# A row sum bound by its loads: all loads issued by SyncE, row buffers and the last runs on aligned addresses

## The chip, the core and the metric

The kernel runs on one core of one Trainium2 chip. The metric is device time in microseconds (us); the lower, the better. The times of before are 160.58, 160.60 and 160.58 us, with a median of 160.58 us.

## The reference

```python
# x: float32 [32, 512, 1024]
def reference(x):
    return np.sum(x, axis=-1).astype(np.float32)
```

The input is 16,384 rows of 1,024 numbers, 64 MiB in all. The output is one number for each row, 64 KiB.

## The kernel before, in words

The 16,384 rows are seen as 128 partitions with 128 rows each (`J = 128`). They are loaded 16 rows per partition at a time (`BIG = 16`), which is 64 KiB in each partition and 8 MiB in all, into three row buffers `rows_0` to `rows_2` that are used in turn. `rows_0` begins at byte 16,512 of each partition, which lies 128 bytes past a multiple of 256; the other two follow at distances of 65,536 bytes. The source of every partition's piece begins at a whole row, so at a multiple of 4,096 bytes.

The order of the work is written out by hand:

1. **The first load** (line 97) brings eight rows per partition, 4 MiB. SyncE (SP) issues it at the program's entry, ahead of the barrier between the engines.
2. **Seven loads of 8 MiB** (`g` from 0 to 6, line 99) follow. GpSimd (POOL) issues them with `single_packet=True`. From `g = 2` on POOL first waits on the semaphore `summed`, which VectorE (DVE) raises when it has summed the block that lies in the buffer to be filled again.
3. **The last eight rows** come as four runs, issued by POOL (line 99) once `summed` shows that their buffer is free. Run 0 is rows 1 to 5 and the first 484 numbers of row 6. Run 1 is row 7 and the first 774 numbers of row 8. Run 2 is the rest of row 6 (540 numbers) and run 3 the rest of row 8 (250 numbers). Runs 2 and 3 land in the small tensor `ends`, runs 0 and 1 in a row buffer. The runs' semaphores are called `five`, `seventh`, `sixth` and `eighth`.

Each load has a semaphore of its own, which reaches 16 when all of it has landed.

DVE sums the first load and loads 0 to 5 with one reduction each (`vec`, line 106). The last big load is split: DVE sums ten of its rows with `halves` (line 115, which adds the two halves of a row and accumulates), and ScalarE (ACT) sums six (`act`, line 135). Of the last eight rows ACT takes three. Rows 6 and 8 are summed in two steps: the part that landed first goes into one element of `ends`, and a second `halves` adds that element, the rest of the row and a zero. Two zeros are written at the start by one strided memset (line 170).

ACT stores the results of the first 112 rows per partition (lines 210 and 211); SP waits for DVE (`done`) and ACT, issues the last store (line 227) and waits until it has landed (line 228).

Of the kernel before, what the change touches and what calls it, by code (L numbers as in the profile page):

```python
# [30 lines left out]
def kernel(  # L31
# [5 lines left out]
    nc = tc.nc  # L37
# [7 lines left out]
    fp32 = mybir.dt.float32  # L45
    P = 128
    batch, seq, dim = x.shape
# [18 lines left out]
    def rows_from(j, n):  # L66
        if j < ONE:
            return x_a[:, j : j + n, :]
        return x_b[:, j - ONE : j - ONE + n, :]

    last = J // BIG - 1
    tail = last * BIG
    FIRST = 8

    bufs = [
        ctx.enter_context(nc.sbuf_tensor(f"rows_{k}", [P, BIG * dim], fp32))
        for k in range(3)
    ]
    sums = ctx.enter_context(nc.sbuf_tensor("sums", [P, J], fp32))
    SIXTH, EIGHTH = 484, 774  # L80
    ends = ctx.enter_context(
        nc.sbuf_tensor("ends", [P, 2 * dim - SIXTH - EIGHTH + 4], fp32)
    )
    unread = [
        ctx.enter_context(nc.psum_tensor(f"unread_{k}", [P, dim], fp32)) for k in range(4)
    ]
# [1 line left out]
    def semaphore(name):  # L88
        return ctx.enter_context(nc.semaphore(name=name))

    def block_of(t, a, n):
        return t[:, a * dim : (a + n) * dim].rearrange("p (n d) -> p n d", d=dim)

    def load(dst, src, k):
        sem = semaphore(f"load_{k}")
        if k == "first":
            nc.sync.dma_start(out=dst, in_=src).then_inc(sem, 16)
        else:
            nc.gpsimd.dma_start(out=dst, in_=src, single_packet=True).then_inc(sem, 16)  # L99
        return sem  # L100

    summed = semaphore("summed")

    def vec(j, block):
        n = block.shape[1]
        return nc.vector.tensor_reduce(  # L106
            out=sums[:, j : j + n],
            in_=block,
            axis=mybir.AxisListType.X,
            op=mybir.AluOpType.add,  # L110
        )

    def halves(dst, src):
        n = src.shape[-1] // 2
        return nc.vector.tensor_tensor_reduce(  # L115
            out=src[:, :n],
            in0=src[:, :n],
            in1=src[:, n:],
            scale=1.0,
            scalar=0.0,  # L120
            op0=mybir.AluOpType.add,
            op1=mybir.AluOpType.add,
            accum_out=dst,
        )
# [21 lines left out]
    t = bufs[0]  # L146
    block = block_of(t, 0, FIRST)
    landed = load(block, rows_from(tail, FIRST), "first")
    loads = [(landed, tail, block)]
    for g in range(last):  # L150
        t = bufs[(1 + g) % 3]
        if g > 1:
            nc.gpsimd.wait_ge(summed, g - 1)
        block = block_of(t, 0, BIG)
        loads.append((load(block, rows_from(g * BIG, BIG), g), g * BIG, block))

# [7 lines left out]
    rows5, left6 = block_of(t, 0, 5), t[:, 5 * dim : 5 * dim + SIXTH]  # L164
    c = 6 * dim
    row7, left8 = t[:, c : c + dim], t[:, c + dim : c + dim + EIGHTH]
    six = dim - SIXTH + 2
    whole6, whole8 = ends[:, :six], ends[:, six:]
    right6, right8 = whole6[:, 1:-1], whole8[:, 1:-1]
    nc.vector.memset(ends[:, six - 1 :: whole8.shape[-1]], 0.0)  # L170
    for landed, first, block in loads[:-1]:
        nc.vector.wait_ge(landed, 16)
        vec(first, block).then_inc(summed, 1)
    nc.gpsimd.wait_ge(summed, last - 1)
    line = rows_from(j, 8).rearrange("p n d -> p (n d)")
    runs = ((t[:, : 5 * dim + SIXTH], 0), (t[:, c : c + dim + EIGHTH], 6 * dim),
            (right6, 5 * dim + SIXTH), (right8, 7 * dim + EIGHTH))
    five, seventh, sixth, eighth = (
        load(dst, line[:, at : at + dst.shape[-1]], f"run_{k}")
        for k, (dst, at) in enumerate(runs)  # L180
    )
# [5 lines left out]
    carried = semaphore("carried")  # L187
    landed, first, block = loads[-1]
# [7 lines left out]
    n_early = n_acts  # L196

    nc.vector.wait_ge(five, 16)
    halves(whole6[:, :1], left6).then_inc(carried, 1)
    for q in range(3):  # L200
        halves(sum_of(q), rows5[:, q, :])
    for q in range(3, 5):
# [10 lines left out]

    done = semaphore("done")
    nc.vector.wait_ge(seventh, 16)
    halves(whole8[:, :1], left8).then_inc(carried, 1)
    nc.vector.wait_ge(sixth, 16)
    nc.vector.wait_ge(carried, 1)
    halves(sum_of(5), whole6)
# [39 lines left out]
```

## Time and profile before

| | |
|---|---|
| median of the runs | 160.58 us |
| span of the profiled execution, first to last instruction | 159.6 us |
| median minus span | 0.98 us |
| DVE busy | 121.6 us, 42 instructions |
| ACT busy | 11.0 us |
| POOL busy | 6.2 us |
| DMA traffic | 67.18 MB, mean 421 GB/s over the span |

The profiled execution has no time of its own beside its span: the span runs from the first to the last instruction, and what a run takes before and after it is not in the profile. The 0.98 us are therefore the difference between that span and the median of the runs.

In the profile, a DMA queue's "share of 16 engines" is the time that its packets took, divided by the length of the stretch and by 16, since every load is spread over 16 DMA engines. A packet is put down to the stretch in which it starts. "q0 software_dynamic" is the queue of the loads that POOL issues, "q1 hardware_dynamic" that of SP's DMAs, "q10" that of ACT's.

### The profile page before, as it was taken

The numbers are of one execution on the slowest core, as the hardware profiler recorded it, in microseconds if no ns is written. First come the engines' busy times: TensorE is split into PE (matmuls) and PEld (weight loads), VectorE is DVE, ScalarE is ACT, GpSimd is POOL, SyncE is SP. The second block draws the span as 40 slices with busy tenths as digits, with TensorE's granted clock in tenths as the row PEclk, the third lists the DMA queues.
The fourth block names the chain that finished last, engine by engine and source line by source line (L and its number), as shares of the span: only waits on it lengthen the run. The fifth ranks groups of instructions, "written<-read, shape, count | busy, mean of one in ns | idle before, by whom it ended". The sixth has DMA issues, their size and how long they took to land.

```text
span 159.6 us, 123 instructions
## 1 busy us (share of the span) xinstructions
DVE 121.6 (76%) x42; ACT 11.0 (7%) x19; POOL 6.2 (4%) x15
## 2 busy tenths in 40 slices
DVE  0000008999998999949999499986999679995986
ACT  3000000000000000000000000000000000000995
POOL 3000000010001000010000100010000220000000
DMA  7999996996997979969969969969969979898993
GB/s 263 526 394 394 435 600 279 526 509 279 526 444 345 526 345 444 526 279 509 526 263 526 526 263 526 509 279 526 509 279 526 460 329 526 378 411 364 438 402 127
DMA packets 2000, 67.18 MB, mean 421 GB/s; under 512 B 624, under 2 KB 624, under 8 KB 848
## 3 DMA queue, kind: packets, MB, share of 16 engines
q0 software_dynamic: 1424, 62.92, 91.2%
q1 hardware_dynamic: 288, 4.20, 6.6%
q10 hardware_dynamic: 288, 0.06, 0.2%
HBM read 67.11 MB, written 0.07 MB: 421 GB/s over the span
## 4 chain that ended last, share of the span: by engine, by line
DMA 74%; DVE 22%; POOL 1%; issue 1%; POOLq 0%
DMA rows<-in_x_dram 56%; DVE sums L106 22%; DMA ends<-in_x_dram 19%; POOL rows L99 1%; DVE ends L115 0%; DVE sums L115 0%; POOLq L43 0%
## 5 line engine op out<-in xcount | busy, mean ns | idle before, releaser
L106 DVE TENSOR_REDUCE sums<-rows 128x16 f32<-128x16384 f32 (+1 forms) x7 | 111.9, 15999 | 32.2 <-DMA rows<-in_x_dram 32.2
L135 ACT ACTIVATE unread<-rows 128x1024 f32<-128x1024 f32 x9 | 9.1, 1013 | 145.5 <-DMA rows<-in_x_dram 145.5
L115 DVE CUSTOM_DVE_ANT_0 rows<-rows 128x512 f32<-128x512 f32 (+2 forms) x15 | 9.0, 659 | 2.6 <-DMA rows<-in_x_dram 2.6
L99 POOL DMA_DIRECT2D rows<-in_x_dram x9 | 4.9, 546 | 122.4 <-DVE sums L106 120.9
L135 ACT ACTIVATION_READ_ACCUMULATOR unread<-rows 128x1 f32 x9 | 1.7, 186 | 0.0
L135 ACT ACT_TABLE_LOAD x1 | 1.3, 1283 | 1.4 <-PEq L43 1.4
L170 DVE MEMSET ends<- 128x2 f32 x1 | 0.1, 60 | 1.5 <-PEq L43 1.5
L115 DVE DVE_READ_ACCUMULATOR2_ANT sums<- 128x1 f32 x15 | 1.2, 80 | 0.0
L99 POOL DMA_DIRECT2D ends<-in_x_dram x2 | 1.1, 543 | 0.0
L115 DVE CUSTOM_DVE_ANT_0 ends<-ends 128x271 f32<-128x271 f32 (+1 forms) x2 | 0.7, 364 | 0.1
L115 DVE DVE_READ_ACCUMULATOR2_ANT ends<- 128x1 f32 x2 | 0.2, 84 | 0.0
L243 POOL MEMSET const-float32-0.0<- 128x1 f32 x1 | 0.1, 99 | 0.2 <-issue 0.2
L243 POOL MEMSET const-bfloat16-1.0<- 128x1 bf16 x1 | 0.1, 103 | 0.0
L243 POOL MEMSET const-float32-1.0<- 128x1 f32 x1 | 0.1, 99 | 0.0
L243 POOL MEMSET const-uint8-127<- 128x1 uint8 x1 | 0.1, 99 | 0.0
## 6 DMA issues: line engine op xcount, KB each, us to landing
rows<-in_x_dram SPq DMA_DIRECT2D x1, 4096.0 KB, 24.5
rows<-in_x_dram POOLq DMA_DIRECT2D x1, 2802.0 KB, 27.9
rows<-in_x_dram POOLq DMA_DIRECT2D x1, 899.0 KB, 29.6
ends<-in_x_dram POOLq DMA_DIRECT2D x1, 270.0 KB, 29.7
ends<-in_x_dram POOLq DMA_DIRECT2D x1, 125.0 KB, 29.5
rows<-in_x_dram POOLq DMA_DIRECT2D x7, 40.5
out_dram<-sums ACTq DMA_DIRECT2D x1, 48.0 KB, 1.6
out_dram<-sums ACTq DMA_DIRECT2D x1, 8.0 KB, 1.5
```

What stands on the lines that cost most here:

```text
L99: nc.gpsimd.dma_start(out=dst, in_=src, single_packet=True).then_inc(sem, 16)
L106: return nc.vector.tensor_reduce(out=sums[:, j : j + n], in_=block, axis=mybir.AxisListType.X, op=mybir.AluOpType.add,)
L115: return nc.vector.tensor_tensor_reduce(out=src[:, :n], in0=src[:, :n], in1=src[:, n:], scale=1.0, scalar=0.0, op0=mybir.AluOpType.add, op ...
L135: nc.scalar.activation(out=unread[n_acts % len(unread)][:, :], in_=src, func=mybir.ActivationFunctionType.Copy, accum_out=sums[:, j : j + ...
L170: nc.vector.memset(ends[:, six - 1 :: whole8.shape[-1]], 0.0)
L243: nc = _bacc.Bacc("TRN2", target_bir_lowering=False, num_devices=1)
```

## The change

SP issues all loads, plain, without `single_packet`; the waits on `summed` that stood ahead of the loads move from POOL to SP with them. A tensor named `unused` fills the space up to the next multiple of 4,096 bytes, so that the row buffers begin at byte 20,480. The runs are cut at 512 and 768 numbers instead of 484 and 774; `ends` now lies directly behind the row buffers, the piece of row 8 in it begins 64 numbers (256 bytes) behind the end of that of row 6, and the partial sum and the zero stand behind each piece instead of around it. The two zeros are written by two memsets.

```diff
+    taken = (nc.sbuf_base + 31) // 32 * 32
+    ctx.enter_context(nc.sbuf_tensor("unused", [P, -taken % 4096], mybir.dt.uint8))
     bufs = [ ... ]
+    SIXTH, EIGHTH = 512, 768
+    PAD = 64
+    ends = ctx.enter_context(
+        nc.sbuf_tensor("ends", [P, 2 * (dim + PAD) - SIXTH - EIGHTH], fp32)
+    )
     sums = ctx.enter_context(nc.sbuf_tensor("sums", [P, J], fp32))
-    SIXTH, EIGHTH = 484, 774
-    ends = ctx.enter_context(
-        nc.sbuf_tensor("ends", [P, 2 * dim - SIXTH - EIGHTH + 4], fp32)
-    )
...
     def load(dst, src, k):
         sem = semaphore(f"load_{k}")
-        if k == "first":
-            nc.sync.dma_start(out=dst, in_=src).then_inc(sem, 16)
-        else:
-            nc.gpsimd.dma_start(out=dst, in_=src, single_packet=True).then_inc(sem, 16)
+        nc.sync.dma_start(out=dst, in_=src).then_inc(sem, 16)
         return sem
...
-            nc.gpsimd.wait_ge(summed, g - 1)
+            nc.sync.wait_ge(summed, g - 1)
...
-    six = dim - SIXTH + 2
-    whole6, whole8 = ends[:, :six], ends[:, six:]
-    right6, right8 = whole6[:, 1:-1], whole8[:, 1:-1]
-    nc.vector.memset(ends[:, six - 1 :: whole8.shape[-1]], 0.0)
+    n6, n8 = dim - SIXTH, dim - EIGHTH
+    right6, right8 = ends[:, :n6], ends[:, n6 + PAD : n6 + PAD + n8]
+    whole6, whole8 = ends[:, : n6 + 2], ends[:, n6 + PAD : n6 + PAD + n8 + 2]
+    left_sums = [w[:, -2:-1] for w in (whole6, whole8)]
+    for w in (whole6, whole8):
+        nc.vector.memset(w[:, -1:], 0.0)
...
-    nc.gpsimd.wait_ge(summed, last - 1)
+    nc.sync.wait_ge(summed, last - 1)
...
-    halves(whole6[:, :1], left6).then_inc(carried, 1)
+    halves(left_sums[0], left6).then_inc(carried, 1)
...
-    halves(whole8[:, :1], left8).then_inc(carried, 1)
+    halves(left_sums[1], left8).then_inc(carried, 1)
```

In bytes per partition the four runs were 22,416, 7,192, 2,160 and 1,000; they become 22,528, 7,168, 2,048 and 1,024. Both add up to 32,768.

## The prediction

> **What bounds the kernel now.** I read the page first: its lines on DVE, DMA, the queues and the chain.
>
> ```profile
> span 159.6 us, 123 instructions
> DVE 121.6 (76%) x42; ACT 11.0 (7%) x19; POOL 6.2 (4%) x15
> ...
> DMA  7999996996997979969969969969969979898993
> ...
> DMA packets 2000, 67.18 MB, mean 421 GB/s; under 512 B 624, under 2 KB 624, under 8 KB 848
> ...
> q0 software_dynamic: 1424, 62.92, 91.2%
> q1 hardware_dynamic: 288, 4.20, 6.6%
> ...
> DMA 74%; DVE 22%; POOL 1%; issue 1%; POOLq 0%
> ```
>
> The two load queues together hold the 16 DMA engines for 97.8% of the span. DVE is busy 76% of it. The chain names DVE for 22%, so the timeline has to tell whether DVE ever holds up a load.
>
> ```profile
> 0.00 0.38 SPq L97 DMA_DIRECT2D rows<-in_x_dram  x1
> ...
> 1.94 1.20 POOL L99 DMA_DIRECT2D rows<-in_x_dram  x2 [1.50 <-POOLq L43]
> 24.48 8.69 DVE L106 TENSOR_REDUCE sums<-rows 128x8 f32<-128x8192 f32 x1 [22.91 <-DMA rows<-in_x_dram]
> ...
> 70.43 17.22 DVE L106 TENSOR_REDUCE sums<-rows 128x16 f32<-128x16384 f32 x1 [2.13 <-DMA rows<-in_x_dram]
> ...
> 126.65 1.05 POOL L99 DMA_DIRECT2D rows<-in_x_dram  x2 [18.82 <-DVE sums L106]
> 127.69 1.08 POOL L99 DMA_DIRECT2D ends<-in_x_dram  x2
> ...
> 147.84 0.69 DVE L115 CUSTOM_DVE_ANT_0 rows<-rows 128x512 f32<-128x512 f32 x1 [2.13 <-DMA rows<-in_x_dram]
> ...
> 157.44 0.44 DVE L115 CUSTOM_DVE_ANT_0 ends<-ends 128x271 f32<-128x271 f32 x1
> ...
> 157.81 0.28 DVE L115 CUSTOM_DVE_ANT_0 ends<-ends 128x126 f32<-128x126 f32 x1
> ...
> 158.13 0.35 SPq L227 DMA_DIRECT2D out_dram<-sums  x1
> ```
>
> It does not. From 70.43 to 147.84 DVE starts four new blocks after the first, always on a landing, so an 8 MiB load takes (147.84 - 70.43) / 4 = 19.35 us, and DVE needs only 17.22 us for it. The last four loads are issued from 126.65 on, 21 us ahead of the landing at 147.84 of the load before them. At 19.35 us for 8 MiB, 64 MiB take 154.8 us; the remaining 4.8 us of the span are the start (the first packets) and the end (last landing, a 0.28 us sum, the store).
>
> Next, single packets, picked out with the DMA view over narrow stretches. In this order the stretches are 0 to 2 us; 5.9 to 6.0; 6.53 to 6.6; 147.4 to 153.4 (run 0); 153.5 to 155.5 (run 1).
>
> ```profile
> q1 hardware_dynamic: 16, 0.52, 96.6%
> ```
> ```profile
> q1 hardware_dynamic: 1, 0.03, 75.8%
> ```
> ```profile
> q0 software_dynamic: 2, 0.13, 432.1%
> ```
> ```profile
> q0 software_dynamic: 112, 2.51, 97.7%
> ```
> ```profile
> q0 software_dynamic: 131, 0.85, 102.0%
> ```
>
> One 32 KiB packet on SP's queue took 0.758 x 16 x 0.1 = 1.213 us, one 64 KiB packet on POOL's 4.321 x 16 x 0.07 / 2 = 2.420 us. Eight of the latter are 19.36 us, the whole period of a load: the packets stand end to end, on one queue, without a gap. Two of the former are 2.426 us, so a packet costs 6 ns beside its bytes, and 2.414 us per 64 KiB, or 36.8 ns per 1,000 bytes, is the rate. The first 16 packets took 0.966 x 2 = 1.93 us each, 0.72 us over the later ones.
>
> **The change part by part.** The sum is made against the span of 159.6 us plus the 0.98 us that separate it from the median, 160.58 us.
>
> *Loads 0 and 1 move to SP's queue.* SP issues them behind its own first load, after the barrier, where POOL did it at 1.94. The first load's eight packets per engine last until about 1 + 1.93 + 7 x 1.21 = 11.4 us, so an issue at 2 us is covered by 9 us: 0. With one queue the first load no longer shares the engines with load 0. It lands near 12 us instead of 24.48, DVE's first sum ends near 21 instead of 33.17, and load 2 is issued earlier. Behind that stand loads 0 and 1, 38 us of transfer, so nothing ends earlier by it: 0.
>
> *The later issues and their waits.* SP now waits for `summed` and issues at 0.38 us a load, where POOL took about 0.53.
>
> ```profile
> POOL rows L99 <- DVE sums L106: 120.9, 6, 30.3
> DVE sums L106 <- DMA rows<-in_x_dram: 32.2, 6, 22.9
> ```
>
> POOL idled 120.9 us on those waits, so they are slack, and on SP nothing else is queued behind them but the final store, due at 158.13, while the last wait ends near 126.4: 0. If the 21 us of cover were gone, a load would start late by DVE's sum; nothing here shortens it.
>
> *64 KiB packets on SP's queue.* The trace shows that queue with 32 KiB packets alone. If it keeps 64 KiB whole: 0. If it halves them, 7 loads x 8 packets = 56 more per engine at 6 ns cost +0.34 us. I take 0, since SP's queue carried the first load's 32 KiB pieces whole.
>
> *Aligned row buffers.* Packets now land 128 bytes past a multiple of 256. The bounds: nothing, or all 6 ns of 56 + 8 + 16 = 80 packets per engine, -0.48 us. The nearest rows are runs 0 and 1, whose ends are crooked too. Run 0: 0.977 x 6 x 16 / 112 = 0.837 us, by the line 22,416 bytes plus 6 ns are 0.832. Run 1: 13 of the 131 are completion writes (under 512 bytes); leaving those 9 ns each, (1.020 x 2 x 16 - 0.12) / 118 = 0.276 against 0.271. So a crooked end costs 5 ns, and run 0 and run 1 regain 16 x 5 ns = -0.08 us. For the shifted begin I take a third of the 6 ns, as part of them must be what any packet costs: -0.14 us.
>
> The Trainium skill (DMA: Bandwidth & Descriptors, section How a descriptor splits into AXI transactions) says that a piece not starting at a multiple of 256 bytes pays the 32-byte beats from the boundary below it. By it a shift of 128 bytes costs 4 beats on 2,048, 0.2% of the transfer, an estimate of -0.3 us when it goes; that lies inside the bounds above, and no run so far shows an aligned load.
>
> *Runs 2 and 3 as single packets.* The page has 848 - 624 = 224 packets from 2 to 8 KB: run 1's 128, so 96 for the 256 pieces of runs 2 and 3, which POOL's queue grouped. On SP's queue each piece is probably a packet: (256 - 96) / 16 = 10 more per engine at 6 ns, +0.06 us. The bytes of the four runs stay.
>
> *The end.* Landing and completion:
>
> ```profile
> ends<-in_x_dram POOLq DMA_DIRECT2D x1, 270.0 KB, 29.7
> ends<-in_x_dram POOLq DMA_DIRECT2D x1, 125.0 KB, 29.5
> ...
> out_dram<-sums SPq DMA_DIRECT2D x1, 8.0 KB, 1.4
> ```
> ```profile
> DMA packets 1, 0.00 MB, mean 0 GB/s; under 512 B 1, under 2 KB 1, under 8 KB 1
> ## 3 DMA queue, kind: packets, MB, share of 16 engines
> q0 software_dynamic: 1, 0.00, 0.2%
> ```
> ```profile
> q1 hardware_dynamic: 1, 0.00, 0.1%
> ```
>
> These last two answers are for 157.24 to 157.5 and for 159.17 to 159.6: the last completion write of the loads on POOL's queue starts after 157.24 and run 3 is known to have landed at about 157.7 (issue near 128.2 plus 29.5), up to 0.5 us later; on SP's queue the store's starts after 159.17 and all is over at 159.6, at most 0.4. Moving the completions to SP's queue may save 0 to 0.1 us; I take -0.05.
>
> ```profile
> L115 DVE CUSTOM_DVE_ANT_0 rows<-rows 128x512 f32<-128x512 f32 x13 | 8.1, 685 | 2.1 <-DMA rows<-in_x_dram 2.1
> L115 DVE CUSTOM_DVE_ANT_0 ends<-ends 128x271 f32<-128x271 f32 x1 | 0.4, 443 | 0.1
> L115 DVE CUSTOM_DVE_ANT_0 ends<-ends 128x126 f32<-128x126 f32 x1 | 0.3, 284 | 0.0
> L170 DVE MEMSET ends<- 128x2 f32 x1 | 0.1, 60 | 1.5 <-PEq L43 1.5
> ```
>
> `halves` costs (685 - 443) / (512 - 271) = 1.0 ns a column. On the path lies only the last one, 129 columns instead of 126, +0.003 us; row 6's falls from 271 to 257. The second memset adds 0.06 us at 1.5 us, hidden in 23 us of waiting (10 after the change).
>
> The sum: 0 + 0 + 0 - 0.08 - 0.14 + 0.06 - 0.05 = -0.21 us, so 160.37, rounded 160.4 us. A measurement of this kernel can tell about 0.2%, 0.32 us, from no change; -0.21 stays within it.
>
> **The rivals.**
>
> *A: alignment is worth its full bound.* All 6 ns per packet were the shift, -0.48 - 0.08 + 0.06 - 0.05 = -0.55 us: 160.0 us. For it: the estimate by the page's rule. Against it: some cost per packet must remain. It decides once a packet gains more than 4 ns. Chance 0.27.
>
> *B: the straggling engine goes with POOL's queue.* One engine runs behind the others. The DMA view of 5.7 to 6.4 and of 157.05 to 157.4:
>
> ```profile
> DMA packets 1, 0.03 MB, mean 47 GB/s; under 512 B 0, under 2 KB 0, under 8 KB 0
> ```
> ```profile
> DMA packets 2, 0.00 MB, mean 9 GB/s; under 512 B 1, under 2 KB 1, under 8 KB 2
> ```
>
> At 5.7 to 6.4 a single engine starts a packet, all others had done so before; at the end one piece and its completion stand alone, about 0.3 us late. Without this, 160.58 - 0.3 = 160.25, and with the sum above 160.05. But the lag is there at 6 us, before POOL's first packet (the 64 KiB ones begin at 6.53): it comes from the first load's slow first packets, which stay. Chance 0.05. The Trainium skill (same page, section Latency and other measured facts) holds that two engines are slowed by the descriptor rings of POOL's path, its best guess; by that rule this rival would be right, and the trace speaks against it.
>
> *C: slower, by gaps between loads on one hardware queue.* On SP's queue the trace shows one load, so no boundary between two loads. If a load's completion write holds the next load's packets until the data have landed, each of the 11 boundaries costs up to the 0.4 us of completion seen above, 4.4 us: 164.8 us. Today another queue could fill such a gap, after the change none can. It decides from (0.32 + 0.21) / 11 = 0.05 us a boundary. Against it: POOL's queue pays nothing there (8 x 2.420 = 19.36 against 19.35). Chance 0.13, with small gaps (161 us) likelier than the full price.
>
> *D: slower, 64 KiB packets are halved and alignment brings nothing.* +0.34 + 0.06 = +0.40: 160.98 us. Chance 0.10.
>
> **How the numbers follow.** The forecast, 160.4 us, has 0.45; its own range is 160.1 to 160.9 (no gain from alignment and a part of D, or 4 ns a packet). Faster by over 0.2%: A and B, 0.32. Slower by over 0.2%: C and D, 0.23. The range is 159.9 to 161.2: it takes in A, B, D and C's small gaps, and leaves out C's full price and a sum of A and B, together some 0.15.
>
> **What would show it.** In the new profile: SP's queue with some 67 MB and no POOL DMA; packets of 64 KiB between 2.410 and 2.420 us; DVE's block starts still 19.3 to 19.35 us apart; the first reduction near 12 us; run 2's and run 3's landings within 0.4 us of each other and the span near 159.4. Twice as many packets would show D, a period above 19.40 us C, one below 19.32 A. It would be wrong altogether if DVE no longer waited about 2 us for each block.

## The result, and the profile after

The changed kernel takes 160.32 us (median of 19 runs, 160.23 to 160.57), the kernel before 160.58 us in the same comparison (160.47 to 160.83). The ratio is 0.998, 95% interval 0.9974 to 0.9985, so 0.24 to 0.42 us are saved. A second comparison, on the chip of most of the experiments, gave 160.38 against 160.67 us, ratio 0.9979 (0.997 to 0.9988). The forecast was 160.4 us.

The page of the changed kernel:

```profile
span 159.0 us, 124 instructions
...
DVE 121.7 (77%) x43; ACT 10.9 (7%) x19; POOL 0.2 (0%) x4
...
DMA packets 2160, 67.18 MB, mean 422 GB/s; under 512 B 624, under 2 KB 752, under 8 KB 1008
...
q1 hardware_dynamic: 1872, 67.12, 98.1%
...
DMA 74%; DVE 24%; issue 0%; SPq 0%
```

All loads are on SP's queue, and the kernel is bound by them as before: one queue fills 98.1% of the span. There are 160 packets more (2,160 against 2,000), as worked out for runs 2 and 3. The timeline:

```profile
12.05 8.69 DVE L106 TENSOR_REDUCE sums<-rows 128x8 f32<-128x8192 f32 x1 [10.45 <-DMA rows<-in_x_dram]
31.36 17.22 DVE L106 TENSOR_REDUCE sums<-rows 128x16 f32<-128x16384 f32 x1 [10.63 <-DMA rows<-in_x_dram]
...
147.50 0.69 DVE L115 CUSTOM_DVE_ANT_0 rows<-rows 128x512 f32<-128x512 f32 x1 [2.19 <-DMA rows<-in_x_dram]
...
156.92 0.43 DVE L115 CUSTOM_DVE_ANT_0 ends<-ends 128x257 f32<-128x257 f32 x1
...
157.27 0.29 DVE L115 CUSTOM_DVE_ANT_0 ends<-ends 128x129 f32<-128x129 f32 x1
```

The first sum starts at 12.05 instead of 24.48, and nothing follows from it. From the start on load 6 to that of the last `halves` it is 157.27 - 147.50 = 9.77 us, against 157.81 - 147.84 = 9.97 before. The DMA view of single stretches (60 to 60.5; run 0 in 146.6 to 152.95):

```profile
q1 hardware_dynamic: 2, 0.13, 60.5%
```
```profile
q1 hardware_dynamic: 144, 2.88, 105.5%
```

A 64 KiB packet lasts 0.605 x 0.5 x 16 / 2 = 2.420 us, whole, and as long as on POOL's queue with the crooked begin. Run 0's 128 packets (16 of the 144 are 9 ns completion writes) last (1.055 x 6.35 x 16 - 0.14) / 128 = 0.836 us for 22,528 bytes, 1 ns over the line of 6 ns plus 36.8 ns per 1,000 bytes.

One plain correction of the span's reading: every later run lists its own time and span, and they are 1.26 to 1.36 us apart for both kernels. The 0.98 us of the prediction put the span of one execution beside the median of others. That execution of before must have taken about 159.6 + 1.3 = 160.9 us. The difference of the two profiled spans (159.6 and 159.0) therefore shows more than the medians do.

### The profile page after: what moved, and what is told of

It is laid out like the page before. It is cut to its first block, busy times and chain, and to the rows that moved or that the text cites. A ratio compares the mean times of both kernels' runs of the same rounds, so it can differ in the third digit from the quotient of the medians.

```text
span 159.0 us, 124 instructions
## 1 busy us (share of the span) xinstructions
DVE 121.7 (77%) x43; ACT 10.9 (7%) x19; POOL 0.2 (0%) x4
## 2 busy tenths in 40 slices
DMA packets 2160, 67.18 MB, mean 422 GB/s; under 512 B 624, under 2 KB 752, under 8 KB 1008
## 3 DMA queue, kind: packets, MB, share of 16 engines
q1 hardware_dynamic: 1872, 67.12, 98.1%
## 4 chain that ended last, share of the span: by engine, by line
DMA 74%; DVE 24%; issue 0%; SPq 0%
DMA rows<-in_x_dram 74%; DVE sums L106 22%; DVE rows L115 2%; SPq L99 0%; DVE ends L115 0%; DVE sums L115 0%
## 5 line engine op out<-in xcount | busy, mean ns | idle before, releaser
L115 DVE CUSTOM_DVE_ANT_0 ends<-ends 128x257 f32<-128x257 f32 (+1 forms) x2 | 0.6, 360 | 0.0
```

Of the source, the lines that this page charges most:

```text
L115: return nc.vector.tensor_tensor_reduce(out=src[:, :n], in0=src[:, :n], in1=src[:, n:], scale=1.0, scalar=0.0, op0=mybir.AluOpType.add, op ...
```

## The experiments

**1. One part at a time.** Four kernels were compared with before on one chip.

*SP alone:* the kernel before with the edit to `load` and the waits, nothing aligned.

```diff
-        if k == "first":
-            nc.sync.dma_start(out=dst, in_=src).then_inc(sem, 16)
-        else:
-            nc.gpsimd.dma_start(out=dst, in_=src, single_packet=True).then_inc(sem, 16)
+        nc.sync.dma_start(out=dst, in_=src).then_inc(sem, 16)
...
-            nc.gpsimd.wait_ge(summed, g - 1)
+            nc.sync.wait_ge(summed, g - 1)
...
-    nc.gpsimd.wait_ge(summed, last - 1)
+    nc.sync.wait_ge(summed, last - 1)
```

> The kernel before with all loads issued by SP; buffers at byte 16,512 and cuts at 484 and 774 as before. Theory 1 (the gain of 0.26 us is the alignment of the four last runs; the queue is worth nothing): 160.55 us, within 0.08 us of before, and from the landing of load 6 to that of run 3 about 9.95 us as before (9.74 after the change). Theory 2 (the queue brings it, by faster completions and by less lag of the slowest engine): 160.3 us, and 9.75 us from load 6 to run 3.

Measured: 160.73 us, ratio 1.0008 (0.9999 to 1.0017). No gain; theory 2 falls.

*Alignment alone:* the changed kernel with that edit undone.

> The changed kernel with its eleven later loads issued by POOL with single_packet again; buffers and cuts aligned. Theory 1 (alignment of the runs): 160.35 us, load 6 to run 3 in about 9.75 us. Theory 2 (queue): 160.58 us, 9.95 us, and one engine about 0.3 us behind the others at every landing again.

Measured: 160.41 us, ratio 0.9984 (0.9975 to 0.9993). The gain is there without SP.

*Filler removed:* rows and `ends` again begin 128 bytes past a multiple of 256.

```diff
-    taken = (nc.sbuf_base + 31) // 32 * 32
-    ctx.enter_context(nc.sbuf_tensor("unused", [P, -taken % 4096], mybir.dt.uint8))
```

> The changed kernel without the filler: row buffers again 128 bytes past a multiple of 256, the cuts stay at 512 and 768. My prediction gave this shift 0.14 us, so 160.46 us. Theory 1b (only the lengths of the runs count; the begin of a row buffer does not, since a load takes 19.35 us with and without the filler): 160.32 us, and load 6 to run 3 in 9.74 us.

Measured: 160.59 us, ratio 0.9997 (0.9989 to 1.0006). Most of the gain is gone, so theory 1b, mine at that point, is wrong: the begin of the buffers counts, and for more than the prediction's 0.14 us.

*Cuts back:*

```diff
-    SIXTH, EIGHTH = 512, 768
+    SIXTH, EIGHTH = 484, 774
```

> The changed kernel with the cuts back at 484 and 774; SP issues, row buffers on 4 KB. Theory 1 and 1b: the gain goes, 160.53 us, run 0's packets 5 ns over the line of bytes, load 6 to run 3 in about 9.95 us. Theory 2 (queue) and the prediction's shift of the row buffers: 160.35 to 160.4 us, load 6 to run 3 at most 9.8 us.

Measured: 160.47 us, ratio 0.9989 (0.998 to 0.9998). Some 0.15 us go, not all. The four agree with one sum: on SP's queue the begin of the buffers is worth 160.73 - 160.47 = 0.26 us with the crooked cuts and, by the ratios, 0.0017 x 160.6 = 0.27 us with the straight ones; the cuts are worth 160.73 - 160.59 = 0.14 us and 0.0009 x 160.6 = 0.14 us. Each of the cuts' two differences is about as large as its uncertainty, so that figure is less sure than the other. With these cuts run 3's pieces in `ends` also begin off a multiple of 256 (2,416 bytes behind those of run 2), so the figure holds a little of the begin.

One expectation failed here: run 0's packets did not last 5 ns over the line of bytes again. The DMA view of the kernel with the cuts back from 150.9 to 153.0, and of the kernel without the filler from 146.7 to 153.0:

```profile
q1 hardware_dynamic: 46, 1.03, 114.0%
```
```profile
q1 hardware_dynamic: 144, 2.88, 106.8%
```

With crooked ends and aligned begins a packet of 22,416 bytes lasts 1.140 x 2.1 x 16 / 46 = 0.833 us; the line says 0.832. (Seven stray packets earlier in run 0, of up to 0.98 us, are left out by this stretch.) With straight ends and shifted begins one of 22,528 bytes lasts (1.068 x 6.3 x 16 - 0.14) / 128 = 0.840 us, where the changed kernel has 0.836. By the records of these traces run 1's packets go the same way: 0.272 us aligned, 0.275 with shifted begins, 0.273 with crooked ends (four strays left out). So the 5 ns that the prediction read off runs 0 and 1 go mostly with the begin, not with the end.

**2. Which boundary counts.** The filler was made longer by 256, 224 and 32 bytes, with the unaltered changed kernel beside it.

```diff
-    ctx.enter_context(nc.sbuf_tensor("unused", [P, -taken % 4096], mybir.dt.uint8))
+    ctx.enter_context(nc.sbuf_tensor("unused", [P, -taken % 4096 + 224], mybir.dt.uint8))
```

> The changed kernel itself, unaltered, on the same chip as the next three, as their point of reference. Expected: 0.26 to 0.32 us below the kernel before, 160.32 us where before is 160.6; the completion writes' distance from their landing stays at 0.32 to 0.35 us from the first load to the last.

Measured: 160.38 us, ratio 0.9979 (0.997 to 0.9988).

> Row buffers and ends 256 bytes past a multiple of 4,096 (byte 20,736); all else as changed. Theory a (multiples of 256 count, 4 KB is not needed): as the unaltered changed kernel within 0.08 us, distance from completion write to landing flat at 0.33 us. Theory b (4 KB counts): 0.2 to 0.3 us above it, as with the shift of 128, and the distance grows from 0.36 to 0.50 us over the program.

Measured: 160.34 us, ratio 0.9978 (0.9969 to 0.9987). Theory a: multiples of 256 are enough.

> Row buffers and ends 224 bytes past a multiple of 256. The shift of 128 cost 0.27 us (160.59 against 160.32). Theory p (each piece pays the 32-byte beats between the boundary and its begin, 7 instead of 4): 0.47 us above the unaltered changed kernel, about 160.8 us. Theory q (each piece that does not begin on a boundary pays the same once): 0.27 us above it, 160.6 us. Either way the distance from completion write to landing grows over the loads.

Measured: 160.66 us, ratio 1.0001 (0.9992 to 1.0009), 0.28 us over the changed kernel.

> Row buffers and ends 32 bytes past a multiple of 256. Theory p (beats up to the begin, 1 instead of 4): 0.07 us above the unaltered changed kernel, 160.4 us. Theory q (the same once for any shift): 0.27 us above it, 160.6 us.

Measured: 160.69 us, ratio 1.0002 (0.9993 to 1.0011), 0.31 us over it. Shifts of 32, 128 and 224 bytes cost the same within what these runs can tell: theory q. Theory p wanted 0.07, 0.27 and 0.47.

Where the time sits is seen when a load's last completion write is set beside the landing that DVE waits for. First the kernel shifted by 32: its timeline at load 0 and load 6, and the DMA view at 31.12 to 31.13 and 147.20 to 147.21, where these loads' last completion writes (under 512 bytes) start.

```profile
31.58 17.22 DVE L106 TENSOR_REDUCE sums<-rows 128x16 f32<-128x16384 f32 x1 [10.67 <-DMA rows<-in_x_dram]
...
147.75 0.69 DVE L115 CUSTOM_DVE_ANT_0 rows<-rows 128x512 f32<-128x512 f32 x1 [2.15 <-DMA rows<-in_x_dram]
```
```profile
DMA packets 3, 0.07 MB, mean 6554 GB/s; under 512 B 2, under 2 KB 2, under 8 KB 2
```
```profile
DMA packets 3, 0.05 MB, mean 4506 GB/s; under 512 B 1, under 2 KB 1, under 8 KB 1
```

The same four of the unaltered changed kernel, its writes at 31.19 to 31.20 and 147.14 to 147.15:

```profile
31.52 17.22 DVE L106 TENSOR_REDUCE sums<-rows 128x16 f32<-128x16384 f32 x1 [10.60 <-DMA rows<-in_x_dram]
...
147.51 0.69 DVE L115 CUSTOM_DVE_ANT_0 rows<-rows 128x512 f32<-128x512 f32 x1 [2.16 <-DMA rows<-in_x_dram]
```
```profile
DMA packets 2, 0.07 MB, mean 6554 GB/s; under 512 B 1, under 2 KB 1, under 8 KB 1
```
```profile
DMA packets 1, 0.00 MB, mean 0 GB/s; under 512 B 1, under 2 KB 1, under 8 KB 1
```

Shifted, DVE starts 0.45 us after load 0's last completion write and 0.54 us after load 6's; unshifted, 0.32 and 0.36 us. Shifted, a load takes (147.75 - 31.58) / 6 = 19.362 us, unshifted (147.51 - 31.52) / 6 = 19.332: 30 ns a load, 0.18 us over six. Of these, only 0.05 us are the growth of that distance (0.09 against 0.04 us). The rest is the pace of the packets themselves: the two completion writes lie 147.20 - 31.12 = 116.08 us apart shifted and 147.14 - 31.19 = 115.95 unshifted. The record of a single 64 KiB packet hardly shows it (2.42 us in both).

The size of the cost is not to be had from one such pair: the first profile of the changed kernel gives (147.50 - 31.36) / 6 = 19.357 us for a load, only 5 ns less than the shifted kernel. The medians give it. An engine gets 96 pieces, 8 of the first load, 56 of the seven big ones and 32 of the four runs, and 0.28 to 0.31 us are some 3 ns for each.

**3. Many more pieces.** Each big load as four DMAs of 16 KiB pieces, on 4 KB and with the filler removed; the waits on a load then ask for 64.

```diff
-        nc.sync.dma_start(out=dst, in_=src).then_inc(sem, 16)
+        if isinstance(k, int):
+            for q in range(0, BIG, 4):
+                nc.sync.dma_start(
+                    out=dst[:, q : q + 4, :], in_=src[:, q : q + 4, :]
+                ).then_inc(sem, 16)
+        else:
+            nc.sync.dma_start(out=dst, in_=src).then_inc(sem, 16)
...
```

> The changed kernel with each of the seven big loads cut into four DMAs of four rows, 16 KiB a partition, on SP's queue; DVE and ACT still wait for all four. That makes 21 more boundaries between DMAs and 168 more packets per engine. The prediction's price of 6 ns a packet: +1.0 us, 161.3 us; its rival C (0.4 us a boundary): +8 us, 168.7 us. Theory of now (packets are recorded 6 to 7 ns longer than they hold their engine, since each begins before the end of the last; a boundary costs one completion write of 6 ns): +0.1 to +0.4 us, 160.4 to 160.7 us.

Measured: 161.26 us, ratio 1.004 (1.0027 to 1.0053). The prediction's 6 ns a packet gave 161.3; my theory of that moment, that a packet is nearly free, is wrong.

> The same with four DMAs per load, row buffers and ends 128 bytes past a multiple of 256, cuts at 512 and 768. If the shift costs each piece the same, four times as many pieces cost four times the 0.27 us of the shift: about 1.0 us above the same kernel on 4 KB, 161.6 us. If the shift costs by the byte or only once in the program: 0.27 us above it, 160.8 us.

Measured: 162.28 us, ratio 1.0102 (1.0087 to 1.0118): 1.02 us over its aligned twin, 3.9 ns for each of now 264 pieces an engine. The shift costs by the piece. The timelines of the two, aligned first:

```profile
31.61 17.22 DVE L112 TENSOR_REDUCE sums<-rows 128x16 f32<-128x16384 f32 x1 [10.77 <-DMA rows<-in_x_dram]
...
148.30 0.69 DVE L121 CUSTOM_DVE_ANT_0 rows<-rows 128x512 f32<-128x512 f32 x1 [2.23 <-DMA rows<-in_x_dram]
```
```profile
31.73 17.22 DVE L110 TENSOR_REDUCE sums<-rows 128x16 f32<-128x16384 f32 x1 [10.87 <-DMA rows<-in_x_dram]
...
149.23 0.69 DVE L119 CUSTOM_DVE_ANT_0 rows<-rows 128x512 f32<-128x512 f32 x1 [2.38 <-DMA rows<-in_x_dram]
```

A load takes 19.448 us aligned and 19.583 us shifted, 135 ns apart over 32 pieces: 4.2 ns a piece. With these pieces the packet records show the shift too. The DMA view of the two from 60 to 80 us, aligned first:

```profile
DMA packets 604, 8.62 MB, mean 431 GB/s; under 512 B 78, under 2 KB 78, under 8 KB 78
...
q1 hardware_dynamic: 604, 8.62, 100.7%
```
```profile
DMA packets 587, 8.47 MB, mean 424 GB/s; under 512 B 70, under 2 KB 70, under 8 KB 70
...
q1 hardware_dynamic: 587, 8.47, 99.5%
```

Without the completion writes of 9 ns each, a 16 KiB packet lasts (1.007 x 20 x 16 - 0.70) / 526 = 0.611 us aligned and (0.995 x 20 x 16 - 0.63) / 517 = 0.615 us shifted, some 3 ns more. These records overlap: 32 of 0.611 us and four completion writes make 19.59 us, where a load takes 19.45. So a packet's record is a little longer than the time that it costs.

Against the changed kernel's 19.332 us, four DMAs cost 116 ns for 24 more packets and 3 more boundaries.

To part packets from boundaries, the next kernel keeps one DMA a load but leaves 256 unused bytes behind every fourth row in the buffer, so that it has as many pieces.

```diff
-        ctx.enter_context(nc.sbuf_tensor(f"rows_{k}", [P, BIG * dim], fp32))
+        ctx.enter_context(nc.sbuf_tensor(f"rows_{k}", [P, BIG * dim + 4 * 64], fp32))
...
+    def gapped(t):
+        return t[:, :].rearrange("p (q r) -> p q r", q=4)[:, :, : 4 * dim]
...
-        loads.append((load(block, rows_from(g * BIG, BIG), g), g * BIG, block))
+        src = rows_from(g * BIG, BIG).rearrange("p (q n) d -> p q (n d)", q=4)
+        loads.append((load(block, src, g), g * BIG, block))
...
```

> The changed kernel with 256 unused bytes behind every fourth row of a big load in the buffers, so that each partition's 64 KiB go into four pieces of 16 KiB, all of them on multiples of 256 bytes, but each load is still one DMA; DVE sums a block with four reductions of four rows. As many packets as the kernel with four DMAs a load (161.26 us), and as many boundaries between DMAs as the changed kernel (160.38 us). Theory n (each packet costs 5 ns): 161.2 us, a load every 19.44 us. Theory m (each boundary between DMAs costs some 40 ns): 160.4 us, a load every 19.34 us.

Measured: 161.80 us, ratio 1.0067 (1.0053 to 1.0081), more than either theory. Its timeline, and its DMA view from 145 to 156:

```profile
31.69 17.40 DVE L109 TENSOR_REDUCE sums<-rows 128x4 f32<-128x4096 f32 x4 [10.70 <-DMA rows<-in_x_dram]
...
148.34 0.69 DVE L118 CUSTOM_DVE_ANT_0 rows<-rows 128x512 f32<-128x512 f32 x1 [2.09 <-DMA rows<-in_x_dram]
...
158.87 0.29 DVE L118 CUSTOM_DVE_ANT_0 ends<-ends 128x129 f32<-128x129 f32 x1
```
```profile
q1 hardware_dynamic: 328, 4.68, 99.6%
q14 instruction: 1, 0.01, 0.2%
```

A load takes (148.34 - 31.69) / 6 = 19.442 us: theory n. 24 packets cost 110 ns, 4.6 ns each (against the 19.357 us of the changed kernel's first profile, 85 ns and 3.5 each); the three boundaries of the kernel with four DMAs are left with 6 ns, 2 ns each, which single executions can't tell from nothing. The rest of the excess comes behind load 6, 158.87 - 148.34 = 10.53 us instead of 9.77. In that stretch one engine also fetched a block of instructions (q14); the only other page that shows such a fetch, that of four DMAs a load, has one of 0.00 MB. This kernel has 18 more DVE instructions. Soon after the fetch a data packet of run 0 lasts far longer than the others; the DMA view from 153.9 to 153.905 shows it alone:

```profile
q1 hardware_dynamic: 1, 0.02, 1708.8%
```

It lasts 17.088 x 0.005 x 16 = 1.367 us instead of 0.836, which is 0.53 of the 0.76 us. That the fetch held it up was not tested.

**4. The queue, with many pieces.** The kernel with four DMAs a load, loads issued by POOL with `single_packet`.

> The kernel with four DMAs a load on 4 KB boundaries (161.26 us, a load every 19.45 us), but with all loads after the first issued by POOL with single_packet, as in the kernel before. Theory 1 (the queue is worth nothing, a packet costs the same 4 to 5 ns on either): 161.2 to 161.3 us, 19.45 us a load. Theory s (POOL's queue groups pieces and so saves packets, as it does with runs 2 and 3): below 160.9 us, 19.34 to 19.40 us a load.

Measured: 161.22 us, ratio 1.004 (1.0026 to 1.0054). SP's was 161.26: theory 1.

## Why the prediction was right

- **What bounds it:** right. Loads still follow one another without a gap, DVE still waits about 2.1 us for each, and its start 12 us earlier brought nothing.
- **Moved issues and waits at 0:** right. SP spent 122.0 us on `summed`, as POOL had spent 120.9:

```profile
SPq L99 <- DVE sums L106: 122.0, 6, 27.5
```

- **64 KiB packets whole on SP's queue, rival D out:** right, 2.420 us each and 1,872 packets in all. The price of D's mechanism, 6 ns a packet, was close: 3.5 to 4.6 ns.
- **The shifted begin, -0.14 us:** right in sign, the mis-sized term. It measured -0.26 to -0.31 us on SP's queue. The step that failed was to give each piece a third of the 6 ns of the packet records, 2 ns, and to count 80 pieces, without those of runs 2 and 3: it is some 3 ns for each of 96 (and 80 times 2 ns would be 0.16, not 0.14). Why a crooked begin costs this, and the same for 32 bytes as for 224, no run here shows.
- **The crooked cuts, -0.08 us:** -0.14 measured, with the uncertainty told above. Its reason failed: the 5 ns over the line in runs 0 and 1 go mostly with the shifted begin, and with an aligned begin a crooked end is left with 1 to 2 ns. Where the rest of what the medians give the cuts comes from is open.
- **Ten more packets, +0.06 us:** about right, +0.05 at 4.6 ns. They come with SP's queue and are in both kernels of each comparison of the cuts.
- **Completions on SP's queue, -0.05 us:** wrong in its reason. The longer distance of the loads' completions from their landings was read as POOL's; SP's shifted loads show it too (0.54 us), SP's aligned ones do not (0.36). With this term, as with the cuts', the alignment's gain was partly counted under the wrong name.
- **The sum, -0.21 us:** measured -0.26, inside the forecast's own range, and in part by luck. The begin and the cuts bring some 0.4 us by the medians, twice what was forecast for them; SP's queue itself is the part left over. SP alone was 0.13 us above before (ten more packets included) in a comparison whose interval still touches no change and reaches 0.27 us, while aligned it was level with POOL's (160.34 to 160.38 against 160.41); so an effect of 0.1 us either way isn't excluded. The gain was also called too small to tell from no change, under 0.32 us; 19 runs of each kernel did tell it.
- **The range:** C's full price and a sum of A and B were said to lie outside it with some 0.15 together. The chances given can't hold that much: all of C has 0.13, and more than half of it lies in small gaps.
- **Rival A, the full bound:** out; about half of the bound came, some 3 ns a piece, where it decides from 4. With 16 KiB pieces the price comes to about these 4 ns.
- **Rival B, the straggling engine:** out. With SP alone, where POOL issues nothing, the DMA view from 5.7 to 6.4 us has two late packets; the changed kernel's has none:

```profile
DMA packets 2, 0.07 MB, mean 94 GB/s; under 512 B 0, under 2 KB 0, under 8 KB 0
```
```profile
DMA packets 0, 0.00 MB, mean 0 GB/s; under 512 B 0, under 2 KB 0, under 8 KB 0
```

  So the lag also comes without POOL's queue, and two kernels that both load by SP alone differ in it. The guess in the Trainium skill (DMA: Bandwidth & Descriptors, section Latency and other measured facts) that POOL's descriptor rings slow an engine doesn't explain it here.
- **Rival C, gaps between loads on one queue:** out; a boundary costs a few ns at most, not 0.4 us.
- **The page's beats** (the Trainium skill, DMA: Bandwidth & Descriptors, section How a descriptor splits into AXI transactions) gave an estimate of -0.3 us, which the measurement met by luck. Its 256-byte boundary is borne out: a shift of 256 is free. Its account by beats is not, for these landings in SBUF: 1, 4 and 7 beats cost the same. The page speaks of bytes that are fetched, and the filler moved only where the bytes land.

## What to carry to other kernels

Where a kernel's time is the time of its DMA packets, count the pieces: here each contiguous piece cost an engine some 4 ns beside its bytes, and 3 to 4 ns more when it began off a multiple of 256 bytes in SBUF. With 64 KiB pieces that is 0.2% of the time, with 16 KiB pieces 0.6%, so the filler is worth its few bytes, and who issues the loads is not worth a change. When a gain is this small, take parts of it apart by making more of them (big loads in four times the pieces made 0.27 us into 1.02), don't size it from one profile of each kernel, and don't set the span of one execution against the median of others.

## What the runs showed that I had not expected

A crooked begin hardly shows in the record of a 64 KiB packet. It shows in the packets' pace, in the records of 16 KiB packets (3 ns), and in part in the landing, which falls behind the packets from 0.45 to 0.54 us over six loads where an aligned kernel stays at 0.32 to 0.36. The cost does not depend on how far off the boundary a piece begins, between 32 and 224 bytes. And a program that grew by 18 instructions showed an instruction fetch among the last packets, with 0.76 us more behind the last big load than the changed kernel.
